# Layer norm with GELU on one core: the first buffer's store as one transfer, and the fourth buffer's load in four pieces

## Chip, cores and metric

One core of one Trainium2 chip runs the kernel. The metric is device time of one execution in microseconds (us). A median is quoted with the number of runs; a ratio is the mean time of one kernel's fast runs over that of the kernel before in the same rounds on the same chip, so it is not quite the ratio of the medians quoted beside it. "Span" is the profiled length of one execution, about 1.8 us less than the measured time. A time in the profile counts from the span's start.

## The reference

```python
# x: 8 x 1024 x 2048 float32; gamma, beta: 2048; eps 1e-5
mean = np.mean(x, axis=-1, keepdims=True)
var = np.var(x, axis=-1, keepdims=True)
normalized = (x - mean) / np.sqrt(var + eps)
out = gamma * normalized + beta
return 0.5 * out * (1 + np.tanh(np.sqrt(2 / np.pi) * (out + 0.044715 * out ** 3)))
```

67.1 MB are read and 67.1 MB written, whatever the order.

## The kernel before

The 8192 rows form 16 buffers (`B`) of 4 MB, each of 128 partitions with `R` = 4 rows of 8 KB. Five slots (`SLOTS`) in SBUF hold them; GELU writes back into the slot, and the store leaves from there. SP issues loads, ACT issues stores. "Row" below is one of the 64 steps of 128 rows of `x` that fill a quarter of a buffer.

```python
def by_row(b):
    return b in (0, B - 1)          # first and last buffer are stored in four row pieces

for b in range(B):                  # SP: loads
    s = b % SLOTS
    if b >= SLOTS:                  # wait until the slot's last store has landed
        prev = sum(16 * (R if by_row(c) else 1) for c in range(s, b, SLOTS))
        sy.wait_ge(s_store[s], prev)
    if b == 0:
        for q in range(R):
            sy.dma_start(out=xts[0][:, q:q + 1], in_=xg[0, :, q:q + 1]).then_inc(s_first[q], 16)
    else:
        sy.dma_start(out=xts[s], in_=xg[b]).then_inc(s_load[s], 16)
...
for t in range(T + 1):              # ACT: normalise row t, then GELU and store of row t - 1
    if t < T:
        ac.activation(out=yks[t % 2], in_=xrow(t), ...)
    i = t - 1
    if i >= 0:
        ac.activation(out=xrow(i), in_=pss[i % 2], func=ACT.Gelu_apprx_tanh)...
        ...
        if by_row(b):
            ac.dma_start(out=og[b, :, q:q + 1], in_=xts[s][:, q:q + 1])...
        elif q == R - 1:
            ac.dma_start(out=og[b], in_=xts[s])...
```

Between the two ACT steps, DVE multiplies by gamma and PE adds beta (a matmul of ones with beta, then one with the identity). DVE also takes the statistics (four `bn_stats` of 512 columns a row, one `bn_aggr`), and POOL turns them into scale and bias.

Of the kernel before, what the change touches and what calls it, by code (L numbers as in the profile page):

```python
# [9 lines left out]

R = 4
SLOTS = 5


@with_exitstack
def kernel(
# [17 lines left out]
    B = T // R  # L34
    xg = xf.rearrange("(b p r) d -> b p r d", p=P, r=R)
# [8 lines left out]
    def sb(name, shape, dt):  # L44
        return pool.tile(shape, dt, name=name)

    xts = [sb(f"xt{s}", [P, R, d], f32) for s in range(SLOTS)]
    yks = [sb(f"yk{s}", [P, d], bf16) for s in range(2)]
# [17 lines left out]
    def sem(name):  # L66
        return tc.alloc_semaphore(name)

    s_first = [sem(f"first{q}") for q in range(R)]
    s_load = [sem(f"load{s}") for s in range(SLOTS)]  # L70
    s_store = [sem(f"store{s}") for s in range(SLOTS)]
    s_par = [sem(f"par{k}") for k in range(3)]
# [9 lines left out]
    def xrow(i):  # L82
        return xts[i // R % SLOTS][:, i % R]

# [6 lines left out]
    def cols(j):  # L91
        return slice(j * FMAX, (j + 1) * FMAX)
# [3 lines left out]
    def v_stats(t):  # L96
        return 3 if t == 0 else 4 + 2 * t + (t - 1)
# [2 lines left out]
        return v_stats(t + 1) + 1 if t + 1 < T else v_stats(T - 1) + 2  # L100

    def by_row(b):
        return b in (0, B - 1)

    with tc.tile_critical():  # L105

        sy = nc.sync
        for b in range(B):
            s = b % SLOTS
            if b >= SLOTS:  # L110
                prev = sum(16 * (R if by_row(c) else 1) for c in range(s, b, SLOTS))
                sy.wait_ge(s_store[s], prev)
            if b == 0:
                for q in range(R):
                    sy.dma_start(out=xts[0][:, q:q + 1], in_=xg[0, :, q:q + 1]).then_inc(s_first[q], 16)
            else:
                sy.dma_start(out=xts[s], in_=xg[b]).then_inc(s_load[s], 16)


        po = nc.gpsimd  # L120
# [18 lines left out]
        def stats(i):  # L139
            xr = xrow(i).rearrange("p (s f) -> p s f", f=FMAX)  # L140
            b, q = divmod(i, R)
            for j in range(nsub):
                ins = ve.bn_stats(out=sts[:, i, j, :], in_=xr[:, j, :])  # L143
                if j == 0 and b == 0:
                    ins._wait_ge(s_first[q], 16)
                elif j == 0 and q == 0:
                    ins._wait_ge(s_load[b % SLOTS], 16 * (b // SLOTS + (b % SLOTS > 0)))
            ins.then_inc(s_v, 1)
            ve.bn_aggr(out=mvs[:, i], in_=sts[:, i])._wait_ge(s_v, v_stats(i) - 1).then_inc(s_v, 1)  # L149

# [5 lines left out]

        ve.memset(b_hl, 0.0).then_inc(s_v, 1)  # L157
        stats(0)

        ve.tensor_tensor(out=split(b_hl[32:33]), in0=row(32), in1=split(b_hl[32:33]),  # L160
                         op=ALU.subtract)._wait_ge(s_c, 2).then_inc(s_v, 1)
        for t in range(1, T):
            stats(t)
            scale(t - 1)
# [11 lines left out]
        for t in range(T + 1):  # L176
            if t < T:
                ac.activation(out=yks[t % 2], in_=xrow(t), func=ACT.Identity, scale=rss[:, t:t + 1],  # L178
                              bias=nms[:, t:t + 1])._wait_ge(s_p, 3 * t + 3).then_inc(s_n, 1)
            i = t - 1  # L180
            if i >= 0:
                ac.activation(out=xrow(i), in_=pss[i % 2],  # L182
                              func=ACT.Gelu_apprx_tanh)._wait_ge(s_t, i + 1).then_inc(s_g, 1)
                b, q = divmod(i, R)
                s = b % SLOTS
                if by_row(b):
                    ac.dma_start(out=og[b, :, q:q + 1],  # L187
                                 in_=xts[s][:, q:q + 1])._wait_ge(s_g, i + 1).then_inc(s_store[s], 16)
                elif q == R - 1:
                    ac.dma_start(out=og[b], in_=xts[s])._wait_ge(s_g, i + 1).then_inc(s_store[s], 16)  # L190
# [4 lines left out]
        for j in range(nsub):  # L195
            ins = pe.matmul(pss[0][:, cols(j)], lhsT=ones[64:65],  # L196
                            rhs=rows[64:65, j * K // nsub:(j + 1) * K // nsub, :d // K], start=True, stop=True)
# [5 lines left out]
        for i in range(T):  # L203
            ps = pss[i % 2]
            for j in range(nsub):
                ins = pe.matmul(ps[:, cols(j)], lhsT=ones_b, rhs=b_hl[:, cols(j)], start=True, stop=False)  # L206
                if j == 0 and i >= 2:
                    ins._wait_ge(s_g, i - 1)
            for j in range(nsub):
                ins = pe.matmul(ps[:, cols(j)], lhsT=ident, rhs=zgs[i % 2][:, cols(j)], start=False, stop=True)  # L210
# [5 lines left out]
        for s in range(SLOTS):  # L216
            sy.wait_ge(s_store[s], sum(16 * (R if by_row(c) else 1) for c in range(s, B, SLOTS)))
# [35 lines left out]
```

## Time and profile before

| | before |
|---|---|
| median of 3 runs | 320.23 us (320.16 to 320.3) |
| span of the profiled run | 318.7 us |
| busiest compute engine | ACT, 79% |
| DMA engines | full in all 40 slices but the ends |

The transfers, and the small queues that carry the engines' own instructions, stand on the page like this (transfers: count, KB each, median us from issue to landing; queues: packets, MB, share of the 16 DMA engines):

```profile
q8 instruction: 4, 0.07, 0.1%
q14 instruction: 6, 0.05, 0.0%
...
xt<-in_x_dram SPq DMA_DIRECT2D x15, 4096.0 KB, 29.1
out_dram<-xt ACTq DMA_DIRECT2D x14, 4096.0 KB, 37.6
out_dram<-xt ACTq DMA_DIRECT2D x8, 1024.0 KB, 14.6
```

A 4 MB transfer alone would take 9.7 us (an estimate: 8 packets of 32 KB on each engine, 1.213 us each in the trace's packet records), so these are times in a queue.

### The profile page before, as it was taken

What the parts mean: (1) busy time and instruction counts of PE and PEld (TensorE: products, weight loads), DVE (VectorE), ACT (ScalarE), POOL (GpSimd) and SP (SyncE); (2) the same over time, 40 slices, a digit from 0 to 9 for tenths busy, and PEclk for the clock granted to TensorE, in tenths of its full rate; (3) what the DMA queues carried; (4) which work ended last, traced back from release to release, by engine and by line L of the source; (5) the groups of instructions that cost most, each with busy time, mean ns of one, the idle gap of its engine ahead of it and who ended that gap; (6) DMA issues with size and microseconds to landing.
All of it is one profiled execution on the core that took longest, in us unless ns stands there. A gap on an engine that the chain in (4) does not pass through costs nothing.

```text
span 318.7 us, 1855 instructions
## 1 busy us (share of the span) xinstructions
PE 241.2 (76%) x510; PEld 57.2 (18%) x520; DVE 249.1 (78%) x386; ACT 252.9 (79%) x132; POOL 115.1 (36%) x201
## 2 busy tenths in 40 slices
PE   2788889889989989785895868859687786768830
PEld 1211112222222222121121111112121121112100
DVE  3688999999999997996869868598786978968610
ACT  2779999999999999796896959949598696977850
POOL 1133444444444444333434424243232452433400
DMA  7999999999999999999999999999999999999995
GB/s 287 440 456 396 427 428 453 409 449 391 411 448 415 449 432 422 441 419 452 419 440 436 419 444 419 446 428 428 444 416 448 419 441 440 415 450 415 448 394 223
DMA packets 6010, 134.36 MB, mean 422 GB/s; under 512 B 704, under 2 KB 752, under 8 KB 752
## 3 DMA queue, kind: packets, MB, share of 16 engines
q1 hardware_dynamic: 2736, 67.11, 49.4%
q10 hardware_dynamic: 3264, 67.14, 49.1%
q8 instruction: 4, 0.07, 0.1%
q14 instruction: 6, 0.05, 0.0%
HBM read 67.13 MB, written 67.11 MB: 421 GB/s over the span
## 4 chain that ended last, share of the span: by engine, by line
DMA 63%; ACT 15%; DVE 9%; POOL 5%; PE 3%; issue 1%; ACTq 1%; SPq 0%
DMA out_dram<-xt 34%; DMA xt<-in_x_dram 27%; ACT yk L178 9%; DVE sts L143 6%; ACT xt L182 5%; POOL rss L131 3%; DVE zg L154 2%; PE ps L196 2%; DMA rows<-in_gamma_dram 2%; POOL ves L129 2%; POOL nms L133 1%; DVE mvs L149 1%; ACT g_t L175 1%; PE ps L210 1%; ACTq L187 0%
## 5 line engine op out<-in xcount | busy, mean ns | idle before, releaser
L143 DVE BATCH_NORM_STATS2 sts<-xt 128x6 f32<-128x512 f32 x256 | 157.7, 678 | 28.9 <-DMA xt<-in_x_dram 28.8
L178 ACT ACTIVATE yk<-xt,nms,rss 128x2048 bf16<-128x2048 f32 x64 | 133.9, 2092 | 44.9 <-POOL nms L133 39.9
L210 PE MATMUL ps<-zg,ident 128*128 128x512 bf16 x246 | 117.7, 627 | 57.2 <-DVE zg L154 55.6
L206 PE MATMUL ps<-b_hl,ones_b 33*128 33x512 bf16 x256 | 120.6, 624 | 2.0 <-ACT g_t L175 2.0
L182 ACT ACTIVATE xt<-ps 128x2048 f32<-128x2048 f32 x64 | 118.8, 1857 | 2.4 <-PE ps L210 2.4
L154 DVE TENSOR_TENSOR zg<-yk,g_t 128x2048 bf16<-128x2048 bf16 x64 | 77.3, 1208 | 20.8 <-ACT yk L178 20.8
L129 POOL TENSOR_SCALAR ves<-mvs 128x1 f32<-128x1 f32 x64 | 29.0, 454 | 172.9 <-DVE mvs L149 172.9
L131 POOL TENSOR_TENSOR rss<-ves,mhalf 128x1 f32<-128x1 f32 x64 | 55.5, 868 | 5.3
L210 PEld LDWEIGHTS ps<-zg,ident 128*128 128x128 bf16 x256 | 27.6, 130 | 147.3 <-DVE zg L154 112.0
L206 PEld LDWEIGHTS ps<-b_hl,ones_b 33*128 33x128 bf16 x256 | 27.1, 127 | 91.9 <-issue 88.4
L133 POOL TENSOR_SCALAR nms<-mvs,rss 128x1 f32<-128x1 f32 x64 | 29.6, 462 | 6.3
L149 DVE BATCH_NORM_AGGREGATE mvs<-sts 128x2 f32<-128x24 f32 x64 | 16.8, 263 | 2.2
L196 PE MATMUL ps<-rows,ones 1*128 1x512 f32 x8 | 7.2, 1072 | 6.1 <-DMA rows<-in_gamma_dram 6.1
L173 ACT ACTIVATE b_hl<-rows 1x2048 bf16<-1x2048 f32 x1 | 1.9, 1908 | 5.1 <-DMA rows<-in_beta_dram 5.1
L160 DVE TENSOR_TENSOR b_hl<-rows,b_hl 1x2048 bf16<-1x2048 f32 x1 | 2.3, 2280 | 2.5 <-ACT b_hl L174 2.5
L196 PEld LDWEIGHTS ps<-rows,ones 1*128 1x128 f32 x8 | 2.5, 322 | 9.3 <-DMA rows<-in_gamma_dram 6.1
L175 ACT ACTIVATE g_t<-ps 128x2048 bf16<-128x2048 f32 x1 | 1.9, 1877 | 2.2 <-PE ps L196 2.2
L169 ACT ACT_TABLE_LOAD x1 | 1.3, 1283 | 0.9 <-SPq L105 0.9
L174 ACT ACTIVATE b_hl<-rows 1x2048 bf16<-1x2048 f32 x1 | 1.9, 1908 | 0.0
L157 DVE MEMSET b_hl<- 33x1024 uint32 x1 | 0.9, 912 | 1.2 <-SPq L105 1.2
L121 POOL MEMSET ones<- 65x128 f32 x1 | 0.2, 201 | 0.5 <-SPq L105 0.5
L125 POOL TENSOR_SCALAR_AFFINE_SELECT ident<-ident 128x128 bf16<-128x128 bf16 x1 | 0.3, 292 | 0.1
(7 smaller groups left out, 0.9 us busy)
## 6 DMA issues: line engine op xcount, KB each, us to landing
xt<-in_x_dram SPq DMA_DIRECT2D x15, 4096.0 KB, 29.1
out_dram<-xt ACTq DMA_DIRECT2D x14, 4096.0 KB, 37.6
out_dram<-xt ACTq DMA_DIRECT2D x8, 1024.0 KB, 14.6
xt<-in_x_dram SPq DMA_DIRECT2D x4, 1024.0 KB, 8.4
rows<-in_beta_dram ACTq DMA_DIRECT2D x2, 8.0 KB, 5.8
rows<-in_gamma_dram ACTq DMA_DIRECT2D x1, 8.0 KB, 5.2
```

Source lines behind the costliest of these rows:

```text
L129: po.tensor_scalar(out=ves[:, c], in0=mvs[:, i, 1:2], scalar1=float(eps), scalar2=1.0, op0=ALU.add, op1=ALU.mult)._wait_ge(s_v, v_stats(i) ...
L131: po.tensor_tensor(out=rss[:, c], in0=ves[:, c], in1=mhalf, op=ALU.pow)._wait_ge(s_p, 3 * i + 1).then_inc(s_p, 1)
L133: po.tensor_scalar(out=nms[:, c], in0=mvs[:, i, 0:1], scalar1=rss[:, c], scalar2=-1.0, op0=ALU.mult, op1=ALU.mult)._wait_ge(s_p, 3 * i + 2 ...
L143: ins = ve.bn_stats(out=sts[:, i, j, :], in_=xr[:, j, :])
L149: ve.bn_aggr(out=mvs[:, i], in_=sts[:, i])._wait_ge(s_v, v_stats(i) - 1).then_inc(s_v, 1)
L154: ve.tensor_tensor(out=zgs[i % 2], in0=yks[i % 2], in1=g_t, op=ALU.mult)._wait_ge(s_n, i + 1).then_inc(s_v, 1)
L175: ac.activation(out=g_t, in_=pss[0], func=ACT.Identity)._wait_ge(s_tg, 1).then_inc(s_c, 1)
L178: ac.activation(out=yks[t % 2], in_=xrow(t), func=ACT.Identity, scale=rss[:, t:t + 1], bias=nms[:, t:t + 1])._wait_ge(s_p, 3 * t + 3).then ...
L182: ac.activation(out=xrow(i), in_=pss[i % 2], func=ACT.Gelu_apprx_tanh)._wait_ge(s_t, i + 1).then_inc(s_g, 1)
L196: ins = pe.matmul(pss[0][:, cols(j)], lhsT=ones[64:65], rhs=rows[64:65, j * K // nsub:(j + 1) * K // nsub, :d // K], start=True, stop=True)
L206: ins = pe.matmul(ps[:, cols(j)], lhsT=ones_b, rhs=b_hl[:, cols(j)], start=True, stop=False)
L210: ins = pe.matmul(ps[:, cols(j)], lhsT=ident, rhs=zgs[i % 2][:, cols(j)], start=False, stop=True)
```

## The change

Its intent is to free slot 0 sooner. The first stores, in 8 KB packets, took turns with loads in 32 KB packets and crawled, so load 5 could only be issued at 63.4 us. Now the store has 32 KB packets and the load in flight at that time (buffer 3) has 8 KB packets.

```diff
+SPLIT = 3
...
     def by_row(b):
-        return b in (0, B - 1)
+        return b == B - 1
...
+            elif b == SPLIT:
+                for q in range(R):
+                    sy.dma_start(out=xts[s][:, q:q + 1], in_=xg[b, :, q:q + 1]).then_inc(s_load[s], 16)
             else:
-                sy.dma_start(out=xts[s], in_=xg[b]).then_inc(s_load[s], 16)
+                sy.dma_start(out=xts[s], in_=xg[b]).then_inc(s_load[s], 16 * R)
...
-                    ins._wait_ge(s_load[b % SLOTS], 16 * (b // SLOTS + (b % SLOTS > 0)))
+                    ins._wait_ge(s_load[b % SLOTS], 16 * R * (b // SLOTS + (b % SLOTS > 0)))
```

## The prediction

> **What bounds the kernel now.** I read the page first, then the chain in order of time, then rates by stretch, then the transfer view of single stretches. The page's opening, its DMA rows and its account of the chain already name the limit:
>
> ```profile
> span 318.7 us, 1855 instructions
> PE 241.2 (76%) x510; PEld 57.2 (18%) x520; DVE 249.1 (78%) x386; ACT 252.9 (79%) x132; POOL 115.1 (36%) x201
> ...
> DMA  7999999999999999999999999999999999999995
> ...
> q1 hardware_dynamic: 2736, 67.11, 49.4%
> q10 hardware_dynamic: 3264, 67.14, 49.1%
> ...
> DMA 63%; ACT 15%; DVE 9%; POOL 5%; PE 3%; issue 1%; ACTq 1%; SPq 0%
> ```
>
> No compute engine is over 79% busy, while the 16 DMA engines are full in every slice but the first and last. The 134 MB that the kernel must read and write are the same after any change of order. The view of busy time by stretch gives the rate (columns: stretch, length, the engines, clock, DMA share, GB/s):
>
> ```profile
> 24.00:58.00 34.00, 29.25 (x64) 6.83 (x64) 31.02 (x49) 31.14 (x17) 15.26 (x24) 1.00 0.99 422
> 58.00:66.00 8.00, 6.88 (x16) 1.71 (x16) 7.43 (x13) 7.40 (x5) 3.95 (x6) 1.00 1.03 438
> 66.00:80.00 14.00, 12.89 (x28) 2.98 (x28) 12.79 (x21) 12.97 (x8) 5.59 (x11) 1.00 1.02 410
> 80.00:280.00 200.00, 157.28 (x339) 36.76 (x344) 165.11 (x259) 165.33 (x88) 77.00 (x130) 1.00 1.00 432
> ```
>
> The settled part moves 432 GB/s; only 24 to 80 us, where stores begin, is below it. At 432 GB/s, 134.3 MB take 310.9 us. The rest of the 318.7 us is the start, the end and this early stretch, so at most some 8 us are there to be won by anything, and only the early stretch is touched by this change. How loads and stores share the engines there is seen in the transfer view of 24 to 58 us (packets, MB, share of the engines):
>
> ```profile
> q1 hardware_dynamic: 385, 11.57, 79.7%
> q10 hardware_dynamic: 371, 2.78, 19.3%
> ```
>
> q1 is the load queue (SP), q10 the store queue (ACT). Both handed out nearly the same number of packets, but the loads' were 32 KB (a partition's four rows) and the stores' 8 KB (one row), so loads got four times the time. This is why the first stores crawl; in the chain the effect is a late slot:
>
> ```profile
> 69.34 29.95 DMA out_dram<-xt
> 99.30 0.02 issue
> 99.31 28.28 DMA xt<-in_x_dram
> ```
>
> From here on the chain is store lands, load follows, load lands, some 8 us of compute, next store: a transfer always waits in a queue of transfers.
>
> **What the Trainium skill says.** "DMA: Bandwidth & Descriptors", section "Queues, rings and completion order": each engine goes round-robin between the queue rows it has work for, at packet granularity. The trace agrees (385 and 371 packets beside each other), except that the page calls a packet 9 to 17 descriptors, and here a turn is one record of 32 or 8 KB. The same page, section "Issuing engines are not separate DMA queues": loads and stores issued by two engines run on the same 16 DMA engines and interleave. Agreed: the two shares add to 99%. The same page, section "Why a DMA increments its semaphore by 16 and not by 1": an increment that is a larger multiple of 16 has its excess added by the sequencer. The changed loads count 64. No trace yet shows the cost, but SP waits for stores for hundreds of us, so it is off the path.
>
> **The change, part by part.** I use packet times from the trace's packet records: 1.213 us for 32 KB, 0.309 us for 8 KB when undisturbed. A 4 MB transfer is 8 packets of 32 KB per engine, 9.70 us alone, or 32 packets of 8 KB, 9.89 us.
>
> Work: three store issues go from ACT and three load issues come to SP. Packets of 8 KB move from four stores to four loads, so their extra 0.19 us for 4 MB cancels. q10 should fall from 3264 packets to 2832 (512 of 8 KB fewer, 128 of 32 KB more, 3 x 16 semaphore writes fewer: 432 less), and q1 rise by the same 432 to 3168. ACT saves three issues of 0.34 us plus gaps; in the timeline only the second and third delayed it, so row 3's GELU ends some 0.8 us sooner, and the first store is issued at about 35.1 us instead of rows at 22.5, 27.3, 31.6 and 35.9. Compute then follows the DVE-POOL loop, so little of it is kept, and none is at the end.
>
> Early order, worked out: loads alone until the store's first packet, 2.4 us after issue (22.5 to 24.9 us before), 37.5 us. Buffer 1 had landed at 23.4; buffer 2 then lands at 33.1, and buffer 3 is 1.8 rows in at 37.5. A store packet of 1.213 us now alternates with a load packet of 0.309 us: eight turns, 12.2 us, so the store of buffer 0 is through at 49.7 and load 5 is issued at about 50 instead of 63.4. Buffer 3 needs 9.8 more packets, to 52.7. Store 1 begins near 54, buffer 4 has then 6.8 packets left, and at equal turns (2.426 us a pair) it lands near 71. Row 16's statistics started at 76.8 before, so compute is not starved. Store 1 lands near 74 (80.3 before), load 5 near 90.5 (88.9 before), store 2 near 93.4 (99.3 before), load 6 near 110 (108.4 before). From there the pattern repeats every 19.4 us as before, with stores some 6 us ahead and loads about 1.7 us behind.
>
> What this is worth: nothing for the bytes. What may be won is what the early stretch lost: 34 us at 422 instead of 432 are 0.8 us, 14 us at 410 are 0.7 us, together 1.5 us. Part is 8 KB packets (moved, not removed: 0.1 us), and part is packets that were slow for no visible cause (about 1.6 us instead of 1.21 near 75 us), which the change need not remove. I choose 40%, 0.6 us: 320.23 - 0.6 = 319.6 us.
>
> The end: loads that land 1.7 us later put the last row's store issue from 308.5 to about 310.2. It needs at least 2.4 us to the first packet, 8 packets of 0.309 us (2.5 us) and 0.3 us to land: 315.4. Before, it landed at 317.3, 8.8 us after issue, behind other stores. If DMA saves 0.6 us it is free only near 316.7, so compute stays hidden, with just over 1 us to spare.
>
> **The rivals.** (1) *The store that waits for row 3 frees its slot later, and the loads starve.* For it: 3 MB of stores that used to start at 22 to 32 us now start at 35. Against it: the old rows landed only at 63.4, and even at equal turns a 4 MB store from 37.5 us needs 19.4 us, to 57. If it had to wait for all loads, it would run from about 52 to 62. In each case work is queued, no engine idles, and the time is 320 us within half a us. (2) *The small load pieces are pushed back too far.* Loads keep a fifth of the engines during the store; if buffer 4 landed 5 us later than I worked out, row 16 would wait, later loads would follow and the end would be set by compute: loads 4 us late instead of 1.7 give a last issue at 312.5, and 5.2 us more plus the 1.4 us that follow the last landing give a span of 319.1, so 320.6 us. (3) *The whole early dip goes,* being caused by rows of stores among long loads and by the gap in loads at 58 to 66 us: 320.23 - 1.5 = 318.7 us. Against it: stores alone moved 438 GB/s there, no worse than the rest, and the slowest packets came after it, with both queues at 32 KB. (4) *ACT's three saved issues count:* 1.1 us, but ACT waits for POOL 39.9 us in all, in steps of up to 3.6 us that are really loads arriving; I give it nothing.
>
> **Range and chances.** Rival 3 whole, with a little of the end besides, gives 318.4; rival 2 with another slow patch of packets gives 320.9. For 2% (6.4 us) to be won nearly all that is not bytes at full rate would have to vanish, start and end included; 2% lost would need idle engines for 6 us, which I find no place for unless the shares go quite otherwise than by packets. So 319.6 us, range 318.4 to 320.9, faster 0.01, same 0.97, slower 0.02.
>
> **What would show it.** Right: q1 at 3168 packets and q10 at 2832; SP's first wait for a store ends near 50 us; the share of loads during that store is near 20%; DMA is full in all slices but the ends; in the settled part 432 GB/s again; loads land 1 to 3 us later and stores about 6 us sooner than before at equal number; DVE still waits for loads nearly 29 us. Wrong: slices of DMA under 9 between 40 and 100 us (rival 1), a wait of row 16 on its load and a last store that finds the queue empty, landing some 5 us after issue (rival 2), or 432 GB/s throughout from 24 us on (rival 3).

## The result

The changed kernel took 320.62 us (median of 4 runs, 320.59 to 320.67), the kernel before 320.26 us (4 runs): ratio 1.001, 95% interval 0.9992 to 1.0027. That is the same within 2%, and a repeat below with more rounds gives 1.004. The page of the changed kernel:

```profile
span 318.8 us, 1865 instructions
...
DMA  7999999999999999999999999999999999999897
...
q1 hardware_dynamic: 3168, 67.11, 49.4%
q10 hardware_dynamic: 2832, 67.13, 49.0%
...
DMA 65%; ACT 15%; DVE 9%; POOL 5%; PE 3%; issue 1%; ACTq 0%; SPq 0%
```

The packet counts are exactly those worked out. DMA is as full as before, except for one slice near the end that reads 8. The view of busy time by stretch, the same stretches as before (last column GB/s):

```profile
24.00:58.00 34.00, 30.34 (x67) 7.09 (x67) 31.20 (x50) 31.80 (x18) 13.52 (x24) 1.00 1.00 418
58.00:66.00 8.00, 7.23 (x17) 1.60 (x16) 7.42 (x12) 7.42 (x5) 3.47 (x6) 1.00 1.04 445
66.00:80.00 14.00, 12.66 (x28) 2.86 (x26) 12.81 (x21) 12.83 (x8) 6.64 (x12) 1.00 0.98 421
80.00:280.00 200.00, 155.58 (x336) 35.90 (x336) 161.15 (x253) 161.31 (x85) 76.20 (x126) 1.00 1.00 433
```

The dip of 66 to 80 us is smaller (421 for 410 GB/s), but 24 to 58 us got worse (418 for 422). Over all 56 us the rate is 422 where it was 421. The mechanism that the change aimed at works, as the transfer view of 40 to 51.5 us shows, during the first store:

```profile
q10 hardware_dynamic: 122, 3.90, 78.7%
q1 hardware_dynamic: 123, 0.88, 18.0%
```

Stores now have four fifths of the engines, again with as many packets as the loads. Load 5 is issued at 52.8 us, 10.6 us sooner, in the timeline of SP, before and then changed:

```profile
63.40 0.33 SPq L117 DMA_DIRECT2D xt<-in_x_dram  x1
```

```profile
52.79 0.35 SPq L121 DMA_DIRECT2D xt<-in_x_dram  x1
```

The chain in order of time shows the price:

```profile
68.07 27.09 DMA out_dram<-xt
95.16 0.02 issue
95.18 34.59 DMA xt<-in_x_dram
129.77 0.02 issue
```

Store 2 lands at 95.2 us (99.3 before), and load 7, issued 4.1 us sooner, lands at 129.8 us, 2.2 us later (127.6 before). By load 15 the lag is 3.5 us: DVE starts on row 60 at 287.0 us, against 283.5. The last store is therefore issued later. First the kernel before, then the changed one, in the timeline of ACT (start, length):

```profile
308.48 0.34 ACTq L187 DMA_DIRECT2D out_dram<-xt  x1
```

```profile
312.00 0.34 ACTq L191 DMA_DIRECT2D out_dram<-xt  x1
```

And store 14, issued at 295.8 instead of 292.3 us, comes after the store queue has run dry. Stretch 293 to 299 us, before and then changed:

```profile
293.00:299.00 6.00, 5.43 (x13) 1.28 (x12) 5.29 (x9) 5.58 (x4) 2.28 (x4) 1.00 1.00 431
```

```profile
293.00:299.00 6.00, 5.28 (x12) 1.15 (x10) 5.04 (x9) 5.58 (x4) 2.47 (x5) 1.00 0.72 306
```

The DMA share falls to 0.72: 28% of 6 us, 1.7 us, is missing from the engines' mean. That looks like the obvious answer: won early, lost late. Experiments had to say whether it is.

### One engine at a time

The mean over 16 DMA engines hides what matters here, and the views don't separate the engines. The trace's packet records do, with a trick: on one engine the next packet starts 3 or 4 ns before the recorded end of the last, so the records can be strung into 16 chains. In the kernel before each chain then has exactly 120 load packets and 112 store packets of 32 KB, as equal shares require (in other runs a chain may be off by a packet where two ends coincide). This gives each engine's last packet and the small reads of instructions that it carried.

| kernel | last engine ends (us) | second last | median engine | 8 KB instruction reads on the last engine, at us |
|---|---|---|---|---|
| before | 316.96 | 316.15 | 314.78 | 43, 132, 232 |
| changed | 317.04 | 316.58 | 316.49 | 43, 134, 235 |

The same kind of engine is last in both: the one that carried three instruction reads. It had no pause near 297 us, because it was behind the others and still busy when they waited. The idle time fell on the other engines, which went on together once store 14 was issued: the median engine ends 1.7 us later than before, the last one 0.1 us later.

### The profile page after: what moved, and what is told of

It reads as the page before. It is cut to its first block, busy times and chain, and to the rows that moved or that the text cites. A ratio compares the mean times of both kernels' runs of the same rounds, so it can differ in the third digit from the quotient of the medians.

```text
span 318.8 us, 1865 instructions
## 1 busy us (share of the span) xinstructions
PE 244.3 (77%) x520; PEld 57.2 (18%) x520; DVE 248.6 (78%) x386; ACT 252.6 (79%) x132; POOL 115.2 (36%) x201
## 3 DMA queue, kind: packets, MB, share of 16 engines
q1 hardware_dynamic: 3168, 67.11, 49.4%
## 4 chain that ended last, share of the span: by engine, by line
DMA 65%; ACT 15%; DVE 9%; POOL 5%; PE 3%; issue 1%; ACTq 0%; SPq 0%
DMA xt<-in_x_dram 33%; DMA out_dram<-xt 30%; ACT yk L182 9%; DVE sts L147 6%; ACT xt L186 5%; POOL ves L133 3%; DVE zg L158 2%; PE ps L200 2%; DMA rows<-in_gamma_dram 2%; POOL rss L135 1%; POOL nms L137 1%; DVE mvs L153 1%; PE ps L214 1%; ACT g_t L179 1%; ACTq L194 0%
## 5 line engine op out<-in xcount | busy, mean ns | idle before, releaser
L147 DVE BATCH_NORM_STATS2 sts<-xt 128x6 f32<-128x512 f32 x256 | 157.7, 679 | 32.6 <-DMA xt<-in_x_dram 32.6
L214 PE MATMUL ps<-zg,ident 128*128 128x512 bf16 x256 | 120.8, 627 | 57.7 <-DVE zg L158 57.0
L133 POOL TENSOR_SCALAR ves<-mvs 128x1 f32<-128x1 f32 x64 | 31.7, 495 | 177.0 <-DVE mvs L153 177.0
L135 POOL TENSOR_TENSOR rss<-ves,mhalf 128x1 f32<-128x1 f32 x64 | 51.8, 809 | 5.3
L137 POOL TENSOR_SCALAR nms<-mvs,rss 128x1 f32<-128x1 f32 x64 | 30.8, 481 | 6.3
```

Source lines behind the costliest of these rows:

```text
L133: po.tensor_scalar(out=ves[:, c], in0=mvs[:, i, 1:2], scalar1=float(eps), scalar2=1.0, op0=ALU.add, op1=ALU.mult)._wait_ge(s_v, v_stats(i) ...
L135: po.tensor_tensor(out=rss[:, c], in0=ves[:, c], in1=mhalf, op=ALU.pow)._wait_ge(s_p, 3 * i + 1).then_inc(s_p, 1)
L137: po.tensor_scalar(out=nms[:, c], in0=mvs[:, i, 0:1], scalar1=rss[:, c], scalar2=-1.0, op0=ALU.mult, op1=ALU.mult)._wait_ge(s_p, 3 * i + 2 ...
L147: ins = ve.bn_stats(out=sts[:, i, j, :], in_=xr[:, j, :])
L214: ins = pe.matmul(ps[:, cols(j)], lhsT=ident, rhs=zgs[i % 2][:, cols(j)], start=False, stop=True)
```

## The experiments

Two theories. **Engine theory:** the end is set by the one DMA engine that loses most time to slow packets and instruction reads; neither kernel changes its bytes, so the time stays. **Tail theory:** the change won something early and gave it back because loads land late and compute sets the end (rival 2 of the prediction). Both predict about 320.6 us, so the time alone can't tell.

### Repeats

The two kernels, unchanged.

> The kernel before, unchanged, for a second profile of it. Two theories are to be told apart in this study. Engine theory: the end is set by the one DMA engine that loses most time to slow packets; bytes and packet costs are the same in both kernels, so the time is too. Tail theory: the changed kernel won a little early and gave it back because loads land 3.5 us later and the last row's store is issued at 312.0 instead of 308.5 us. This run: 320.2 to 320.6 us. Engine theory: slow packets (about 2.2 us a DMA engine over what undisturbed packets take) return, at nearly the same times if they belong to the kernel's order, at others if they are chance. In both theories load 15 lands near 283.5 and the last store is issued near 308.5 us.

320.45 us, one look, beside 320.3 us (median of 11). Load 15 lands at 283.5, the last store is issued at 308.5 us. The last engine again carried reads at 43, 132 and 232 us and ended at 316.90 us; the median engine ended at 314.57. Slow packets (recorded time above 1.213 us for 32 KB and 0.309 us for 8 KB) total 1.75 us an engine instead of 2.20: the stretch 60 to 80 us has 0.47 us where it had 0.99. So the size of the dip that the prediction hoped to save varies from profile to profile. That it is there does not: slow packets at 60 to 80 us cost 0.47 to 1.15 us an engine in all seven profiles with the old order (the variants below included), and 0.05 to 0.06 us in all seven with the new store, the new load or both.

> The changed kernel, unchanged, in five rounds, to fix the difference that 1.001 with its interval left open, and for a second profile. Engine theory: ratio 1.000 to 1.001, total of slow packets again near 2.1 us a DMA engine, whatever their times. Tail theory: ratio 1.001, last store issued near 312 us and landing 5.4 us later, some 1.5 us of idle DMA near 297 us.

321.2 us (6 runs, 320.77 to 323.18) against 320.3: ratio 1.0041 (1.0018 to 1.0065). The last store was issued at 312.6 us and landed 5.4 us later; the idle time near 297 us was there. The last engine is the one with reads at 43, 135 and 235 us, at 317.65 us. Slow packets total 2.37 us an engine, of which 0.73 us in 36 to 42 us, exactly where the first profile has 0.74. This repeat is slower than the engine theory expected, and two of its runs (322.53 and 323.18) are a separate matter that no profile caught.

### Each part alone

```diff
-SPLIT = 3
+SPLIT = -1
```

> Only the first part of the change: buffer 0 stored as one 4 MB transfer, load 3 whole. Store and load packets are both 32 KB, so the store of buffer 0 takes equal turns: from about 37.5 to 57 us, load 5 issued near 57.5 (52.8 with both parts, 63.4 before). Loads then land near the times of before or 1 us sooner, the last store is issued near 308 us and waits behind others, so no idle DMA near 297. Engine theory: ratio 0.999 to 1.001. Tail theory: 0.997 to 0.999, the early gain without the late loss.

320.35 us (5 runs) against 320.3: ratio 0.9993 (0.9982 to 1.0005). Load 5 is issued at 60.2 us, row 60 starts at 281.5 us, the last store is issued at 306.5 us, and there is no idle time near 297. So it has an early gain (load 5 is 3.2 us, row 60 2.0 us sooner) without the late loss that the tail theory blames. It wins 0.07%, where that theory said 0.1 to 0.3%, but the interval reaches 0.18%, and the second series below gives 0.14%: this pair of runs does not decide between the theories. Slow packets at 36 to 42 us cost 0.73 us an engine here too. Last engine: reads at 44, 130 and 230 us, end at 316.23; median engine 314.24.

```diff
     def by_row(b):
-        return b == B - 1
+        return b in (0, B - 1)
```

> Only the second part: load 3 in four row pieces, buffer 0 stored by rows as before. From about 33 us both sides have 8 KB packets and take equal turns; the rows' stores are through near 51 us and load 5 is issued then. Loads land 1 to 3 us later than before. Engine theory: ratio 0.999 to 1.001. Tail theory: 1.000 to 1.001, with the last store issued at 310 to 312 us.

320.13 us (5 runs) against 320.3: ratio 0.9995 (0.9983 to 1.0007). Load 5 is issued at 52.2 us, row 60 starts at 285.5, the last store is issued at 310.4 us. The engines that were ahead pause for up to 0.7 us near 295 us. Last engine: reads at 42, 133 and 233 us, end at 316.60. Each part alone is as good as the kernel before; issues of the last store from 306.5 to 310.4 us make no difference.

The store alone was run once more:

> The first part of the change alone, once more, as it was the only version below the kernel before (0.9993, interval across 1). It has 32 packets of 8 KB fewer for each DMA engine, worth 0.2 us, and the same three instruction reads on the slowest engine. Engine theory: 0.999 to 1.000. A win of more than 0.2% would say that the order of early stores matters after all.

319.95 us (5 runs) against 320.35: ratio 0.9986 (0.9973 to 1.0). Both series together suggest that it is about 0.1% faster, 0.3 us, of which 0.2 us would be its fewer 8 KB packets (an estimate: 32 packets of 0.309 us cost 9.89 us, 8 of 1.213 us 9.70); each interval reaches 1, so the gain itself is not shown. If one is to be kept, it is this, though by too little to matter. This series' one profile fell in its slowest run (320.55 us), with the engine of the three reads last at 317.0.

### More and less compute in the tail

One idle activation on ACT ahead of the last three rows:

```diff
+    idle_t = sb("idle_t", [P, d], bf16)
...
         for t in range(T + 1):
+            if t == T - 3:
+                for _ in range(1):
+                    ac.activation(out=idle_t, in_=g_t, func=ACT.Identity)
```

> The kernel before with one idle activation of 128x2048 (some 2 us) on ACT ahead of the last three rows. The last store should be issued near 310.6 instead of 308.5 us. If the end is set by the slowest DMA engine, which never idles, and an issue needs only 5.4 us to land (as in the changed kernel), 310.6 + 5.4 is 316.0, below the 317.3 at which it landed, so nothing moves: ratio 0.999 to 1.002. If compute set the end here too: 1.006.

320.51 us (4 runs) against 320.44: ratio 0.9996 (0.9979 to 1.0013). The last store is issued at 310.4 us, 1.9 us later, and nothing moves.

> The changed kernel with the same idle activation. If its last store has no slack left (issued at 312.0 to 312.6, landing 5.4 us later with the DMA engines waiting), the 2 us go to the end in full: 322.7 to 323.4 us, ratio 1.008 to 1.010. If the slowest DMA engine alone sets the end: 320.6 to 321.2 us, ratio 1.001 to 1.004.

321.05 us (4 runs) against 320.44: ratio 1.0023 (1.0002 to 1.0044), not 1.008. The last store is issued at 313.9 us:

```profile
313.90 0.34 ACTq L195 DMA_DIRECT2D out_dram<-xt  x1
```

It lands at 317.76 us, only 3.9 us after its issue. Now every engine pauses in the tail, the one with DVE's reads included (by 0.1 us), and all 16 end within 0.2 us of each other. Here compute sets the end for the first time, and it needed 1.9 us more to get there. The changed kernel still had some 1.5 us of slack (3.9 us after 312.0 is 315.9 us, against 317.4 us at which its store landed). The tail theory's decisive number fails.

Less work for the last buffer, which makes its values wrong (relative error 0.16):

```diff
-            for j in range(nsub):
+            m = nsub // 2 if i >= T - R else nsub
+            for j in range(m):
...
-            ve.bn_aggr(out=mvs[:, i], in_=sts[:, i])
+            ve.bn_aggr(out=mvs[:, i], in_=sts[:, i, :m])
...
-                ac.activation(out=yks[t % 2], in_=xrow(t), ...)
+                h = slice(0, d // 2 if t >= T - R else d)
+                ac.activation(out=yks[t % 2][:, h], in_=xrow(t)[:, h], ...)
```

> The kernel before with less compute for the last buffer, wrong on purpose there (statistics of half a row, normalised half row). The last store should be issued some 4 to 5 us sooner. Bytes and DMA order until then are the same. Both theories: nothing moves, ratio 0.999 to 1.001, as the last store already waits behind others.

320.57 us (4 runs) against 320.44: ratio 1.0 (0.9985 to 1.0015), with the last store issued at 304.5 us. As expected by both.

> The changed kernel with the same lean tail, wrong on purpose there. Last store issued near 307.5 us, store 14 some 2 us sooner, so the idle DMA time near 297 us shrinks or goes. Tail theory: it falls to 319.5 to 320.3 us, ratio 0.997 to 1.000 against 1.004. Engine theory alone: it stays at 320.6 to 321.2 us, ratio 1.001 to 1.004.

320.84 us (4 runs) against 320.44: ratio 1.0015 (0.9994 to 1.0035). The last store is issued at 308.1 us, 3.9 us sooner, and the pause is gone, as the stretch 293 to 299 us of this run shows:

```profile
293.00:299.00 6.00, 6.00 (x15) 1.43 (x14) 4.42 (x9) 5.07 (x5) 2.94 (x6) 1.00 1.01 431
```

431 GB/s, as in the kernel before, and the end does not move: the last engine, again the one with three reads, ends at 317.09 us (317.04 with the pause), while the median engine ends at 314.55 instead of 316.49. So neither the late loads nor the idle 1.7 us set the time of the profiled run. This is what the engine theory says and the tail theory forbids. (The ratio alone is less sharp: its interval just reaches the 0.997 to 1.000 of the tail theory.)

### The reads of instructions

If one engine sets the end by its three reads, then more reads on it must lengthen the kernel, and fewer reads elsewhere must not shorten it. Whose instructions are they? DVE has 386 in the profile, and three reads of 8 KB would be 384 instructions of 64 bytes; the runs below bear this out (128 DVE instructions fewer take away one 8 KB read, 512 PE instructions fewer two 16 KB reads). 360 more DVE instructions, of one element each, where DVE waits anyway:

```diff
+    tiny = sb("tiny", [1, 9 * 40], f32)
...
             b, q = divmod(i, R)
+            if b >= 7 and q == 0:
+                for e in range(40):
+                    k = (b - 7) * 40 + e; ve.memset(tiny[:, k:k + 1], 0.0)
```

> The kernel before with 360 more DVE instructions, memsets of one element, 40 ahead of the first row of each buffer from 7 on, where DVE waits some 3 us for the load anyway. In every trace so far one DMA engine carries three 8 KB reads of instructions (near 43, 132 and 232 us), each beside a packet slowed by 0.5 us, and it is the one that ends last among the engines in the kernel before; by their spacing they are DVE's instructions, 128 in 8 KB. Engine theory: two or three more such reads on the same engine, 1.6 to 2.5 us, and the end follows: ratio 1.005 to 1.008. If the span depends on bytes or on compute alone: 1.000 to 1.001.

323.24 us (4 runs) against 320.19: ratio 1.0096 (1.0081 to 1.0111), somewhat more than the 1.005 to 1.008 expected. The page of this run has three more instruction reads (6 before), and the group of memsets shows how little DVE had to do for them (count, busy us, mean ns, then its idle time before):

```profile
q14 instruction: 9, 0.07, 0.1%
```

```profile
L145 DVE MEMSET tiny<- 1x1 f32 x360 | 4.8, 59 | 0.0
```

All six reads of DVE (43, 130, 167, 207, 246 and 286 us) are on the same engine. It ends at 319.56 us; the next ends at 316.61 and the median at 315.02. Of the 3.05 us that the time grew, the engine's end explains 2.6: 0.9 us for a read. In this run a read itself takes 0.309 to 0.313 us, and the packet after it on the engine is slowed by 0.48 to 0.65 us. The last store was issued at 310.2 us, later than before but within what the tail runs showed to be free.

> The kernel before with two of four statistics instructions a row, wrong on purpose: 128 DVE instructions fewer and so one instruction read fewer. Engine theory: the last engine ends some 0.8 us sooner, until the next slowest sets the end: ratio 0.997 to 0.998. Otherwise 1.000, since faster compute in the tail of this kernel did nothing.

```diff
-            for j in range(nsub):
+            m = nsub // 2
+            for j in range(m):
```

(with the aggregation cut to match; wrong, relative error 0.02). 319.82 us (5 runs) against 320.19: ratio 0.9984 (0.9971 to 0.9996). One read fewer:

```profile
q14 instruction: 5, 0.04, 0.0%
```

DVE's engine, with reads at 54 and 196 us, ended at 315.51 us and was no longer last; another one, at 316.31, was. The gain is smaller than the 0.2 to 0.3% expected, because the next engine takes over after 0.6 us.

> The kernel before without the 256 bias matmuls, wrong on purpose: 512 fewer PE instructions, whose reads (16 KB each, on other DMA engines) become fewer. Engine theory: those engines had time to spare, so ratio 0.999 to 1.001. If fewer instruction reads help wherever they are: 0.997 to 0.999.

```diff
+            if i >= 2:
+                pe.wait_ge(s_g, i - 1)
...
-                ins = pe.matmul(ps[:, cols(j)], lhsT=ones_b, rhs=b_hl[:, cols(j)], start=True, stop=False)
...
-                ins = pe.matmul(ps[:, cols(j)], lhsT=ident, rhs=zgs[i % 2][:, cols(j)], start=False, stop=True)
+                ins = pe.matmul(ps[:, cols(j)], lhsT=ident, rhs=zgs[i % 2][:, cols(j)], start=True, stop=True)
```

(wrong: no beta). 320.8 us (5 runs) against 320.19: ratio 1.0012 (1.0 to 1.0025), just above the engine theory's 0.999 to 1.001 and clear of the 0.997 to 0.999 of the other case. Here the other queue has two reads fewer and q14 is as it was:

```profile
q8 instruction: 2, 0.03, 0.0%
q14 instruction: 6, 0.05, 0.0%
```

The last engine has reads at 43, 131 and 231 us and ends at 317.27; the median engine is at 314.03, the earliest of all runs. Relieving engines that have time gives nothing. In these runs it is not the number of instructions that counts but which DMA engine carries their reads.

### What the change did on the engine that ends last

The same chains, cut by time, add what the means over 16 engines hide. Slow packets on the engine with DVE's three reads (us over undisturbed time; those right after a read included):

| profiles | 20 to 80 us | after 80 us | of the latter, not after a read |
|---|---|---|---|
| before (2), and with idle activation, lean tail or no beta | 2.09, 1.70; 1.98 to 2.30 | 1.11 to 1.18 | 0.00 to 0.08 |
| changed (2), and with idle activation or lean tail | 1.21, 1.36; 1.28, 1.31 | 1.92 to 2.29 | 0.84 to 1.22 |
| store alone (2) | 1.27, 2.00 | 1.22, 1.23 | 0.00 to 0.01 |
| split alone | 1.50 | 1.21 | 0.01 |

In the pairs of unaltered profiles the changed kernel won 0.6 us early on this engine (1.29 for 1.90 in the mean), and lost 0.8 to 1.1 us after 80 us, most of it (0.72 to 0.95 us) in store packets that took 0.05 to 0.15 us too long, mostly one in each round of 19.4 us. The early figures vary (1.27 and 2.00 in the two profiles of the store alone), so the 0.6 is rough; the late ones do not overlap. So something was won early and lost late after all, though not by compute in the tail. It happens with both parts together and with neither alone; why these packets are slow the runs don't show.

## Why the prediction was right, and where not

The time lay in the range (318.4 to 320.9) and the call "same" held; the repeat's median, 321.2, is 0.3 us above the range. The stated direction, 0.6 us faster, did not hold. That the time stayed so near that of the kernel before is in part luck: on the engine that ends last an early gain and a late loss of about the same size met.

- **Bound by DMA, bytes unchanged:** right. But the bound was described as the mean of 16 engines. What ends the kernel is the last of them, some 2 us after the median in the kernel before.
- **Turns by packet, 4 to 1 for the store:** right. The shares were 78.7% and 18.0%, the packet counts 3168 and 2832. Load 5 was issued at 52.8 instead of 50 us. The store was issued at 35.4 us (35.1 foreseen), but its first packets started at 39.2 to 40.4 us on the 16 engines instead of 37.5; the eight turns then took 11.5 us (12.2 foreseen) on most. The "2.4 us after issue (22.5 to 24.9 us before)" was a misreading: in the kernel before, the first store packets started at 25.9 to 27.4 us.
- **Loads 1.7 us later, stores 6 us sooner:** half right. The median engine's last load packet ends 1.9 us later (281.39 for 279.45). DVE waits for the last engine, and there the lag was 3.7 us (285.44 for 281.75): in the changed kernel the engine with DVE's reads, in the kernel before that engine and another within 0.02 us. The working had one engine for all. Stores 1 and 2 were 4.5 and 4.1 us sooner, not 6, and DVE waited 32.6 us for loads, not nearly 29.
- **The step that failed: "From there the pattern repeats every 19.4 us as before",** and with it the net 0.6 us. On the engine that ends last the early stretch gave what was chosen, 0.6 us in the mean of two profiles each, but slow packets after 80 us, which the working did not have, took back 0.8 to 1.1 us (table above).
- **"I choose 40%, 0.6 us"** of what the early stretch loses was too much for the engines' mean. Slow packets between 20 and 80 us cost 1.34 us an engine in the first profile of before, 0.78 in the second, and 0.96 and 0.92 in the two of the changed kernel. Most of them moved instead of going: they gather at 36 to 42 us (0.74), as the first store joins the loads. In the split alone 0.88 us lies at 20 to 36 us, mostly at 32 and 33 us, where its small load pieces start among the row stores. The 0.7 us of 66 to 80 us did belong to the order of transfers, but its size varies, and the new order pays elsewhere.
- **The end, "compute stays hidden, with just over 1 us to spare":** right, although its two terms were off. The last store was issued at 312.0 instead of 310.2 us, and an issue needs 3.9 us to land, not 5.2 (with idle engines its first packet started after 0.8 us, not 2.4). The measured slack is some 1.5 us.
- **Rival 2** (320.6 us) gave the measured number for the wrong reason: its late issue came, at 312.0 where it said 312.5, and so did the sign named for it, a last store landing some 5 us after issue (5.4), but it did not set the end. The 320.6 is luck besides: it adds 1.5 us to a span of 319.1, where measured time and span of the same run differ by 1.8, which gives 320.9.
- **Rivals 1, 3 and 4:** right to give 1 and 4 nothing; DMA stayed full between 40 and 100 us. Rival 3, the whole dip gone, did not come: 422 GB/s from 24 to 80 us.

**What stays open.** With five rounds the changed kernel was 0.4% slower than before, and its single runs scatter up to 323.2 us, where the kernel before stayed under 321.2. Its two profiled runs explain 0.1 and 0.75 us through the last engine (317.04 and 317.65 for 316.96 and 316.90). That each part alone has no such loss fits the table above, where only both together slow that engine's packets after 80 us. What slows them, and whether the same makes the runs of 322.5 and 323.2 us, is not shown: neither of these was profiled.

## What to carry to other kernels

When DMA is full from end to end, a new order of transfers can only win what is idle or slow, and slow packets may move with the order instead of going: profile the kernel before twice before counting a dip as winnable, and look for new losses long after the stretch that was changed. A transfer ends with its slowest DMA engine (DVE started on the changed kernel's last load at 287.0 us, 1.6 us after the slowest engine's last packet and 5.6 us after the median's), so look at engines one by one before explaining the end by means: an idle 1.7 us in the mean of the engines cost nothing here, and 0.9 us on the one that ends last cost 0.9. To learn whether compute matters at the end, lengthen and shorten it there by a few us; both take a few lines.

## What the Trainium skill lacked or had wrong

- "Runtime: NRT & Kernel Launch", section "Instruction fetch mechanics": it says instruction memory is refilled in 16 KiB blocks and that the cost is mostly hidden. The runs show 16 KB reads in the queue that shrank when PE instructions were removed (4 to 2), but 8 KB for DVE (128 instructions; 3 reads for 386, 6 for 746). The waits of the kernel before put no wait of DVE down to them, but in this kernel, bound by DMA, their cost is not hidden: all of DVE's reads ran on one DMA engine, some 0.9 us each (0.309 for the read, 0.48 to 0.65 for the packet after it), and three more of them made the kernel 0.96% slower.
- "DMA: Bandwidth & Descriptors", section "Queues, rings and completion order": a packet is called 9 to 17 descriptors, and it is the unit of a turn. Here a turn is one record of 8 or 32 KB (how many descriptors that is, the records don't tell): 122 store packets stood beside 123 load packets while their bytes were 3.90 to 0.88 MB. So in these runs the length of a transfer's contiguous row decided its share against the other queue, which the section does not say.
- The same page, section "Latency and other measured facts": it names DMA engines that are usually slower and gives descriptor rings of the software path as its best guess. This kernel has no such path, and its slowest engine was the one that carried DVE's instructions, in all runs but the two that gave it one read fewer or made all engines wait for compute. Which number that engine has, the records don't tell.
- The same page, section "Why a DMA increments its semaphore by 16 and not by 1": it says that the sequencer adds the excess of a larger increment, but for this chip not what that costs. The runs agree and give the cost: each load with 64 issued once DMA was under way shows 17 updates, the first some 0.5 us after its issue; the issue took 0.35 instead of 0.33 us.
- No page that I read says that packets slow down where loads and the first stores begin to mix: 0.68 to 0.81 us an engine at 36 to 42 us in every profile of the changed kernel and of the store alone, 0.70 us at 30 to 36 us in the split alone, and in the two profiles of the kernel before 0.25 and 0.29 us at 20 to 36 us with another 0.47 and 0.99 us at 60 to 80 us. The runs don't show the cause.
